# x loaded into the slots of the residual sums, Exp put right behind Ln, and RWKV pairs with grouped y products and joint key transposes

## The chip, the cores and the metric

The kernel runs on one core of one Trainium2 chip. The metric is the device time of one execution in microseconds; less is better. The times of before are those of three runs.

## What is computed

The reference runs two blocks on x (512 rows of 1024 columns), in fp32. Only the first block is touched. Its core:

```python
mod = silu(c) @ ada_w + ada_b
shift, scale, gate = split(mod, 3)
h = rmsnorm(x, norm_g) * (1.0 + scale) + shift
p = h @ w_in
y_rwkv = rwkv7_group(p[..., :RWKV_COLS], ...)     # 8 heads of 64
y_sb = stick_breaking_group(p[..., RWKV_COLS:], sb_norm_g)   # 8 heads of 64
y = concatenate([y_rwkv, y_sb]) @ w_out
x = x + gate * y
return rmsnorm(x, final_g)
```

`rwkv7_group` carries a 64x64 state per head over the 512 positions:

```python
sa = einsum('bhij,bhj->bhi', state, -kk_t)
state = state * w_t + sa * b_t + v_t * k_t
y_t = einsum('bhij,bhj->bhi', state, r_t)
```

The second block (two layers, the first with a short convolution and a second stream `ctx` of 256 rows, the second with neighbourhood attention, both with a feed-forward part) follows on the result.

## The kernel before, in words

Activations lie with the columns on the partitions (8 k-tiles of 128 by 512 positions). The large fp32 products (GEMMs) are made of three products each, with operands cut into a high and a low part (L172 to L174): per output tile of 128 columns and k-tile three matmuls of 512 positions. `fetch` (L165 to L168) loads weights on SP's queue into `st` (two buffers), ScalarE makes the high part `wh` (L155), VectorE the low part `wl` (L156), four buffers each.

Eight heads of each kind are worked off in pairs. `rwkv_pair` computes the recurrence by chunks of 64 positions, in NCH = 8 steps; `sb_pair` the stick-breaking attention in four row blocks of 128, the last of 512 columns. Their order is the tuple ORDER (L21): an RWKV pair is a generator that is advanced in three pieces, and stick-breaking pairs stand between. The program's text sets only priorities: a list scheduler of the Tile framework puts the instructions of each engine in one fixed order, so that pieces of several pairs, GEMMs among them, stand interleaved. Each engine's queue is worked in that order.

In an RWKV pair the two heads e = 0, 1 lie on partitions 0 to 63 and 64 to 127 (`hs[e]`). The keys of each head are transposed chunk by chunk (L1031) into `BK[e]`. Then come the steps: first state product (L1057, L1059), solve (L1064), new state (L1070, L1074 to L1077), and the output of the step: per head a product of 128 rows (L1081, `SV` by `MMt`), and one of 64 rows (L1083, the old state `VS` by `RA`), which add up in PSUM bank `py`. L1086 copies the bank; L1088, L1093 and L1098 are the norm's sums, and L1099 to L1102 end the pair. `rsqrt` (L240) makes Ln (L242) and Exp (L248) on ScalarE; these two lie in one activation table, the sigmoids of the stick-breaking blocks in another, and each change loads a table.

PSUM banks in the first block: `acc` two (GEMMs), `sm`, `sc`, `py`, `ss`, `sp` and `so` one each.

The output projection goes by eight column blocks m. For each the first six k-tiles (y0, y4, y1, y5, y2, y6, in the order YORD) are multiplied while the last RWKV pair (y3) and the last stick-breaking pair (y7) are still running; for m = 0 to 5 the sum is put out of PSUM at L421 as `part` = sum * gate + x, into the slot of a y that has been split (L307) into its high and low part. x comes from six tiles `xt` of the pool "tail" (L402 to L404), which is opened in the space of the closed pool `rk`, the RWKV pairs' working tiles: a load waits until the tile that lay there is read out. m = 6 and 7 stay in PSUM. Then `w_out2` brings the last two k-tiles (y3, y7) of all eight blocks (L444 to L452), and L461 takes the first sum of squares of the next norm. Beside it the contexts of the second block are loaded (`xc`, L407) and modulated (`nt`, L287; `hc`, L288 to L290).

Of the kernel before, what the change touches and what calls it, by code (L numbers as in the profile page):

```python
# [8 lines left out]
F32 = mybir.dt.float32  # L9
F32R = mybir.dt.float32r  # L10
BF16 = mybir.dt.bfloat16
AF = mybir.ActivationFunctionType
# [5 lines left out]
S = 512  # L18
# [4 lines left out]
CH = 64  # L23
NCH = S // CH
YORD = (0, 4, 1, 5, 2, 6, 3, 7)
# [59 lines left out]
class K:  # L85
# [154 lines left out]
    def rsqrt(self, t, ps, after=None, scale=1.0, eps=0, since=None, out=None, view=None):  # L240
        nc = self.nc
        i = nc.scalar.activation(t, ps, AF.Ln, scale=scale, bias=self.eps[:, eps:eps + 1])  # L242
        if after is not None:
            self.order(i, self.table(after))
        if since is not None:
            self.order(i, since)
        src, dst = (t, t) if out is None else (view[1](t), view[0](out))
        return nc.scalar.activation(dst, src, AF.Exp, scale=-0.5)  # L248

    def sumsq(self, xs, n, pool, tag, psum, scale=None):  # L250
        nc = self.nc
# [57 lines left out]
    def block1(self):  # L309
        nc, tc, A = self.nc, self.tc, self.A  # L310
# [8 lines left out]
        y = [None] * 8  # L319
# [3 lines left out]
        with self.open(name="n1", bufs=2) as npool:  # L323
# [16 lines left out]
            for ch in range(4):  # L340
                pm = self.psum(("py", "sp")[ch % 2])
                for kp in range(4):
                    st = npool.tile([128, 2, 512], F32, tag="ast", name="ast", bufs=16)
                    nc.sync.dma_start(st, A["ada_n"][ch, kp])
                    for i in range(2):
                        k = 2 * kp + i
                        r = slice(32 * (k % 4), 32 * (k % 4) + 32)
# [4 lines left out]
                for i in range(4):  # L352
                    nc.tensor.matmul(tr[:, j + i:j + i + 1], lhsT=ev[:, 128 * i:128 * i + 128], rhs=self.C("sel"),
                                     start=True, stop=True)
# [23 lines left out]
        with self.open(name="sb", bufs=1) as sb:  # L378
            with self.open(name="rk", bufs=1) as rk:
                self.rk, self.sb = rk, sb  # L380
                pl = pre[12]
                zl = rk.tile([128, S], F32, name="zl")
                self.mix(pl, self.V("mu", 12), omu[:, 12:13], zl)
                nc.scalar.activation(zl[0:64], zl[0:64], AF.Tanh)
                self.y = y
                runs = [self.rwkv_pair(p, W, h, zl, omu, oka, pre) for p in range(4)]
                for n in ORDER[:-1]:
                    if n < 4:
                        next(runs[n], None)
                    else:  # L390
                        y[n] = self.sb_pair(n - 4, W, h, sb)
            self.xp = self.pool("xp", side="right")
            self.cxp = self.pool("cxp", side="right")
            self.hcp = self.pool("hc", side="right")
            self.xas = ExitStack()
            xa = self.xas.enter_context(self.open(name="xa", bufs=1, side="right"))
            y[7] = self.sb_pair(3, W, h, sb)
            if self.dbg:
                for k in range(8):
                    nc.sync.dma_start(A['dbg_y'][k], y[k])  # L400
            with self.open(name="tail", bufs=2) as tp:
                xts = [tp.tile([128, S], F32, name=f"xt{m}", bufs=1) for m in range(6)]  # L402
                for m in range(6):
                    nc.sync.dma_start(xts[m], A["x"][m // 2, :, m % 2])  # L404
                xc = self.xc = [self.cxp.tile([128, SC], F32, tag=f"xc{k}", name=f"xc{k}") for k in range(KT)]
                for k in range(KT):
                    nc.sync.dma_start(xc[k], A["ctx"][k])  # L407
                hc = self.hc = [self.hl(self.hcp, SC, f"hc{k}") for k in range(KT)]
                gc = self.gain("gc0", "norm_mix0", mod, 8, 1)
                pc = self.psum("py")[:, :SC]  # L410
                self.sumsq(xc, SC, tp, "c", pc)
                rstd = tp.tile([128, SC], F32, name="rstd", bufs=1)
                since = self.rsqrt(rstd, pc, since=self.sbexp)
                self.modulate(xc, range(KT), gc, mod, 0, 1, hc, tp, "cz", rstd)
                yh, part = [], []
                for k in YORD:
                    if k == 3:
                        for m in range(6):
                            po = self.xgemm(A["w_out"][m], yh, 0, 6)
                            t = self.yp.tile([128, S], F32, tag=f"y{YORD[m]}", name="part")  # L420
                            nc.vector.scalar_tensor_tensor(t, po, self.m1[:, 16 + m, 0:1], xts[m],  # L421
                                                           op0=ALU.mult, op1=ALU.add)
                            part.append(t)
                        for m in (6, 7):
                            po = self.psum("acc")
                            self.gemm(po, A["w_out"][m], yh, 0, 6, last=False)
                            part.append(po)
                        w2 = self.load_w(A["w_out2"][0], 1024) + self.load_w(A["w_out2"][1], 1024)
                    t = self.hl(self.hp, S, f"h{k}")
                    self.split(t, y[k])  # L430
                    yh.append(t)
        xs = self.xs = [xa.tile([128, S], F32, tag=f"x{k}", name=f"x{k}") for k in range(KT)]
        for k in (6, 7):
            nc.sync.dma_start(xs[k], A["x"][k // 2, :, k % 2])
# [10 lines left out]
        for n, m in enumerate((6, 7, 0, 1, 2, 3, 4, 5)):  # L445
            po, base = (part[m], xs[m]) if m >= 6 else (self.psum("acc"), part[m])
# [13 lines left out]
            if n >= 5:  # L460
                nc.tensor.matmul(ms, lhsT=self.C("ones") if n == 5 else fwt[:, n - 6], rhs=acc if n == 5 else sq,  # L461
                                 start=n == 5, stop=n == 7)
# [443 lines left out]
    def rwkv_pair(self, p, W, h, zl, omu, oka, pre):  # L906
        nc, rk = self.nc, self.rk
        TT, STT = nc.vector.tensor_tensor, nc.vector.scalar_tensor_tensor
        mm = nc.tensor.matmul
# [3 lines left out]
        sm = lambda: self.psum("sm", name="rsm")  # L913
# [17 lines left out]
        sg, a = T("t1"), T("t2")  # L931
# [18 lines left out]
        f = T("t1")  # L950
        nc.vector.tensor_scalar(f, a, self.V("k_a", p), oka[:, p:p + 1], op0=ALU.mult, op1=ALU.add)
        XY = T("XY", (128, NCH, 2, CH), 2)
        RA = T("RA", (128, NCH, 2, CH), 2)
        tb = T("tb", bufs=2)
        for e in range(2):
            r = slice(64 * e, 64 * e + 64)
# [8 lines left out]
        MMt = [T(f"MM{e}", (128, NCH, CH), 2) for e in range(2)]  # L965
# [5 lines left out]
        hs = [slice(0, 64), slice(64, 128)]  # L971
        for e in range(2):
            ro, rt = hs[e], hs[1 - e]
# [13 lines left out]
        for c in range(NCH):  # L987
            for q in range(4):
                ro, cl = hs[q // 2], slice(32 * (q % 2), 32 * (q % 2) + 32)
# [34 lines left out]
        TT(XY, XY, PP[:, :, CH:CH + 1].unsqueeze(3).to_broadcast([128, NCH, 2, CH]), ALU.mult)  # L1024
        yield
        BK = [T(f"BK{e}", (128, NCH, CH)) for e in range(2)]
        for e in range(2):
            ro = hs[e]
            pB = self.psum("sm", (128, NCH, CH), "pB")
            for c in range(NCH):  # L1030
                nc.tensor.transpose(pB[:, c], XY[ro, c].rearrange("p a t -> p (a t)"),  # L1031
                                    self.C("ident")[ro, 64 * e:64 * e + 64])
            nc.scalar.copy(BK[e], pB)
        VS = [T(f"VS{e}", (128, NCH, CH)) for e in range(2)]
        SV = [T(f"SV{e}", (128, NCH, CH)) for e in range(2)]
        for w0 in range(0, 9, 4):
# [10 lines left out]
            nc.scalar.copy(VS[1][0:64, w0 - 1 + s0:w0 + n - 1], pV[0:64, s0:n, 64:128])  # L1047
            nc.scalar.copy(SV[1][0:64, w0 - 1 + s0:w0 + n - 1], pV[0:64, s0:n, 64:128])

        pY = self.psum("py")  # L1050
        slots = self.psum("sc", (128, 8, CH))
        for c in range(NCH):
            pR = slots[:, (3 * c + 0) % 8]
# [13 lines left out]
            if c < NCH - 1:  # L1067
# [3 lines left out]
                for e in range(2):  # L1071
# [3 lines left out]
                    else:  # L1075
                        STT(VS[e][r, c + 1], VS[e][r, c], PP[r, c, CH:CH + 1], pS[r],
                            op0=ALU.mult, op1=ALU.add)  # L1077
            for e in range(2):
                r = hs[e]
                o = pY[r, c * CH:c * CH + CH]  # L1080
                mm(o, lhsT=SV[e][:, c], rhs=MMt[e][:, c], start=True, stop=c == 0)  # L1081
                if c > 0:
                    mm(o, lhsT=VS[e][r, c], rhs=RA[r, c, 0, :], start=False, stop=True)  # L1083

        ys = T("BK0")
        nc.scalar.copy(ys, pY)  # L1086
# [188 lines left out]
```

## Time and profile before

| | us |
|---|---|
| median of three runs | 2110.76 |
| lowest and highest | 2107.98, 2111.87 |
| profiled execution, its own time | 2105.49 |
| its span in the trace | 2103.7 |
| TensorE busy | 2051.8 (98%) |
| VectorE busy | 1231.9 (59%) |
| ScalarE busy | 795.2 (38%) |
| GpSimd busy | 131.5 (6%) |
| mean HBM traffic | 96 GB/s |
| mean granted TensorE clock | 0.986 |

The trace is that of one execution, which was 5.3 us faster than the median. Its span lacks 1.8 us of its time, what lies ahead of the first and behind the last recorded instruction. A row of the table of windows shows for a stretch of the span the busy time and the count of instructions of each engine; a row of the timeline shows start, duration, engine, line and operation (and in brackets the idle time before it, with what ended it). A row of the groups shows busy time, mean duration of one, and the idle time before.

### The profile page before, as it was taken

What the parts mean: (1) busy time and instruction counts of PE and PEld (TensorE: products, weight loads), DVE (VectorE), ACT (ScalarE), POOL (GpSimd) and SP (SyncE); (2) the same over time, 40 slices, a digit from 0 to 9 for tenths busy, and PEclk for the clock granted to TensorE, in tenths of its full rate; (3) what the DMA queues carried; (4) which work ended last, traced back from release to release, by engine and by line L of the source; (5) the groups of instructions that cost most, each with busy time, mean ns of one, the idle gap of its engine ahead of it and who ended that gap; (6) DMA issues with size and microseconds to landing.
All of it is one profiled execution on the core that took longest, in us unless ns stands there. A gap on an engine that the chain in (4) does not pass through costs nothing.

```text
span 2103.7 us, 33543 instructions
## 1 busy us (share of the span) xinstructions
PE 2051.8 (98%) x13596; PEld 1651.6 (79%) x13596; DVE 1231.9 (59%) x2641; ACT 795.2 (38%) x1485; POOL 131.5 (6%) x212
## 2 busy tenths in 40 slices
PE   6999999998999999999999999999999999999999
PEld 3766666655888888888888888898777787888887
DVE  2969887645777756767456443354566655434443
ACT  3536444345422224221222122244777744323232
POOL 0000000000000000001001000000233200000000
PEclk9999999987999999999999999999999999999999
DMA  7432313112243421445234322222111122333333
GB/s 279 147 111 83 111 53 98 40 56 81 71 129 122 130 81 45 147 127 174 90 123 155 114 91 60 61 81 71 43 59 61 36 66 92 95 100 96 94 99 102
DMA packets 61356, 203.60 MB, mean 97 GB/s; under 512 B 6928, under 2 KB 8976, under 8 KB 61200
## 3 DMA queue, kind: packets, MB, share of 16 engines
q1 hardware_dynamic: 45360, 145.77, 21.3%
q0 software_dynamic: 15120, 55.06, 8.1%
q8 instruction: 107, 1.75, 0.3%
q10 hardware_dynamic: 720, 0.62, 0.1%
q14 instruction: 49, 0.40, 0.1%
HBM read 199.32 MB, written 2.10 MB: 96 GB/s over the span
## 4 chain that ended last, share of the span: by engine, by line
PE 87%; ACT 3%; DVE 3%; issue 1%; POOL 0%; POOLq 0%; ACTq 0%; DVEq 0%
PE acc L173 19%; PE acc L172 19%; PE acc L174 19%; PE cacc L174 5%; PE cacc L173 5%; PE cacc L172 5%; PE py L895 2%; PE pT L875 2%; PE ss L1147 1%; PE so L1169 1%; PE sm L862 1%; PE py L1083 1%; PE sm L863 1%; PE py L1081 1%; PE ss L1162 1%
## 5 line engine op out<-in xcount | busy, mean ns | idle before, releaser
L155 ACT CAST wh<-st 128x512 fp32r<-128x512 f32 (+2 forms) x481 | 292.3, 609 | 729.8 <-PE acc L173 287.7
L156 DVE TENSOR_TENSOR wl<-st,wh 128x512 fp32r<-128x512 f32 (+2 forms) x481 | 323.1, 674 | 353.9 <-ACT wh L155 350.7
L172 PE MATMUL acc<-xzzh,wh 128*128 128x512 f32 x352 | 138.8, 394 | 0.0
L174 PE MATMUL acc<-xzzh,wl 128*128 128x512 f32 x352 | 138.1, 392 | 0.0
L173 PE MATMUL acc<-xzzl,wh 128*128 128x512 f32 x352 | 138.0, 392 | 0.0
L210 DVE CUSTOM_DVE_ANT_0 junk<-ast,cb,vec 128x512 bf16<-128x512 f32 x168 | 125.2, 745 | 14.5 <-DMA ast<-in_w_ada_dram 11.9
L210 DVE CUSTOM_DVE_ANT_0 junk<-ast,cb,m 128x512 bf16<-128x512 f32 x168 | 125.5, 747 | 2.8
L200 POOL DMA_DIRECT2D ast<-in_w_ada_dram x96 | 50.6, 528 | 1022.3 <-DVE m L210 957.2
L174 PEld LDWEIGHTS acc<-xzzh,wl 128*128 128x128 f32 x352 | 66.0, 188 | 14.8
L172 PEld LDWEIGHTS acc<-xzzh,wh 128*128 128x128 f32 x352 | 66.1, 188 | 13.6 <-issue 0.5
L173 PEld LDWEIGHTS acc<-xzzl,wh 128*128 128x128 f32 x352 | 66.1, 188 | 13.4 <-issue 0.5
L172 PE MATMUL acc<-h0h,wh 128*128 128x512 f32 (+1 forms) x164 | 65.8, 401 | 6.0 <-DVE part L421 3.1
L173 PE MATMUL cacc<-czzl,wh 128*128 128x256 f32 x240 | 68.1, 284 | 0.0
L172 PE MATMUL cacc<-czzh,wh 128*128 128x256 f32 x240 | 67.7, 282 | 0.0
L174 PE MATMUL cacc<-czzh,wl 128*128 128x256 f32 x240 | 67.3, 280 | 0.0
L174 PE MATMUL acc<-h2h,wl 128*128 128x512 f32 (+1 forms) x164 | 65.8, 401 | 0.0
L173 PE MATMUL acc<-h1l,wh 128*128 128x512 f32 (+1 forms) x164 | 65.7, 401 | 0.0
L173 PE MATMUL acc<-h3l,wh 128*128 128x512 f32 (+1 forms) x164 | 65.3, 398 | 0.3 <-DVE h3l L290 0.3
L173 PE MATMUL acc<-h6l,wh 128*128 128x512 f32 (+1 forms) x164 | 65.5, 399 | 0.1
L173 PE MATMUL acc<-h0l,wh 128*128 128x512 f32 (+1 forms) x164 | 65.4, 399 | 0.0
L174 PE MATMUL acc<-h0h,wl 128*128 128x512 f32 (+1 forms) x164 | 65.3, 398 | 0.1
L174 PE MATMUL acc<-h1h,wl 128*128 128x512 f32 (+1 forms) x164 | 65.2, 398 | 0.0
(731 smaller groups left out, 5576.1 us busy)
## 6 DMA issues: line engine op xcount, KB each, us to landing
ast<-in_w_ada_dram POOLq DMA_DIRECT2D x96, 512.0 KB, 3.8
st<-in_ffn_w_in_dram SPq DMA_DIRECT2D x88, 512.0 KB, 3.4
st<-in_ffn_w_out_dram SPq DMA_DIRECT2D x32, 448.0 KB, 3.3
st<-in_w_in_dram SPq DMA_DIRECT2D x24, 512.0 KB, 3.5
st<-in_conv_w_in_dram SPq DMA_DIRECT2D x24, 512.0 KB, 3.6
ast<-in_ada_n_dram SPq DMA_DIRECT2D x16, 512.0 KB, 9.0
st<-in_ffn_w_out_dram SPq DMA_DIRECT2D x16, 512.0 KB, 3.5
st<-in_w_qk_dram SPq DMA_DIRECT2D x16, 512.0 KB, 3.5
```

The lines of the kernel that those rows point to most:

```text
L155: nc.scalar.copy(hi[:, :n], sl)
L156: nc.vector.tensor_tensor(lo[:, :n], sl, hi[:, :n].bitcast(F32), ALU.subtract)
L172: mm(out, lhsT=lh, rhs=rh, start=first, stop=False)
L173: mm(out, lhsT=lh, rhs=rl, start=False, stop=False)
L174: return mm(out, lhsT=ll, rhs=rh, start=False, stop=last)
L200: self.nc.gpsimd.dma_start(st, src)
L210: i = self.nc.vector.tensor_tensor_reduce(out=junk, in0=st[:, hs], in1=c[:, hs], scale=0.5, scalar=o if hf else self.V(bname, j), op0=ALU. ...
L862: mm(o, lhsT=qh[:, e, qs], rhs=ks, start=True, stop=False)
L863: mm(o, lhsT=ql[:, e, qs], rhs=ks, start=False, stop=True)
L875: nc.tensor.transpose(pT[:, to], s[:, 128 * i:128 * i + 128], self.C("ident"))
L895: self.nc.tensor.matmul(po[r, cs], lhsT=v[:, r], rhs=pts[e][:, blk:blk + n].rearrange("p a t -> p (a t)"), start=i == 0, stop=i == len(wor ...
L1081: mm(o, lhsT=SV[e][:, c], rhs=MMt[e][:, c], start=True, stop=c == 0)
```

## The change

Four edits, all in the first block:

1. In `rsqrt` the Exp is issued at high priority, so that the scheduler may set it right behind its Ln.
2. The six `xt` tiles and their loads are gone. Right behind the split of the k-th y (k in YORD) the slot of that y is taken as `part`, and x is loaded into it (L431); the evacuation (L418) reads x there and writes the sum in its place.
3. The keys of both heads are transposed at once: two groups of four 128x128 transposes, and four copies of 256 columns, in place of sixteen 64x128 transposes and two copies of 512.
4. The y products are written behind the steps c = 3 and 7, for four steps at a time: first all products of 128 rows (L1082), then all of 64 rows (L1085). In the PSUM bank only the first step's product starts a sum and only the last step's product ends it.

```diff
-        return nc.scalar.activation(dst, src, AF.Exp, scale=-0.5)
+        with self.tc.high_priority():
+            return nc.scalar.activation(dst, src, AF.Exp, scale=-0.5)
...
-                xts = [tp.tile([128, S], F32, name=f"xt{m}", bufs=1) for m in range(6)]
-                for m in range(6):
-                    nc.sync.dma_start(xts[m], A["x"][m // 2, :, m % 2])
...
-                            t = self.yp.tile([128, S], F32, tag=f"y{YORD[m]}", name="part")
-                            nc.vector.scalar_tensor_tensor(t, po, self.m1[:, 16 + m, 0:1], xts[m],
+                            nc.vector.scalar_tensor_tensor(part[m], po, self.m1[:, 16 + m, 0:1], part[m],
                                                            op0=ALU.mult, op1=ALU.add)
-                            part.append(t)
...
                     yh.append(t)
+                    m = len(part)
+                    if m < 6:
+                        t = self.yp.tile([128, S], F32, tag=f"y{k}", name="part")
+                        nc.sync.dma_start(t, A["x"][m // 2, :, m % 2])
+                        part.append(t)
...
-        for e in range(2):
-            ro = hs[e]
-            pB = self.psum("sm", (128, NCH, CH), "pB")
-            for c in range(NCH):
-                nc.tensor.transpose(pB[:, c], XY[ro, c].rearrange("p a t -> p (a t)"),
-                                    self.C("ident")[ro, 64 * e:64 * e + 64])
-            nc.scalar.copy(BK[e], pB)
+        for hf in range(2):
+            pB = self.psum("sm", (128, 4, 2, CH), "pB")
+            for c in range(4):
+                nc.tensor.transpose(pB[:, c].rearrange("p a t -> p (a t)"),
+                                    XY[:, 4 * hf + c].rearrange("p a t -> p (a t)"), self.C("ident"))
+            for e in range(2):
+                nc.scalar.copy(BK[e][:, 4 * hf:4 * hf + 4], pB[:, :, e])
...
-            for e in range(2):
-                r = hs[e]
-                o = pY[r, c * CH:c * CH + CH]
-                mm(o, lhsT=SV[e][:, c], rhs=MMt[e][:, c], start=True, stop=c == 0)
-                if c > 0:
-                    mm(o, lhsT=VS[e][r, c], rhs=RA[r, c, 0, :], start=False, stop=True)
+            if c % 4 == 3:
+                for d in range(c - 3, c + 1):
+                    for e in range(2):
+                        mm(pY[hs[e], d], lhsT=SV[e][:, d], rhs=MMt[e][:, d], start=d == 0, stop=False)
+                for d in range(max(c - 3, 1), c + 1):
+                    for e in range(2):
+                        mm(pY[hs[e], d], lhsT=VS[e][hs[e], d], rhs=RA[hs[e], d, 0, :], start=False, stop=d == NCH - 1)
```

The scheduler moves instructions with it. Three places:

SP's queue at the end of the first block, before (`st` are weights, `xt` and `x` tiles of x, `xc` of the contexts):

```order
L167 DMA st<-in_w_out_dram 128x768 x6
L404 DMA xt_5143<-in_x_dram 128x512
L404 DMA xt_5144<-in_x_dram 128x512
L404 DMA xt_5145<-in_x_dram 128x512
L404 DMA xt_5146<-in_x_dram 128x512
L404 DMA xt_5147<-in_x_dram 128x512
L404 DMA xt_5148<-in_x_dram 128x512
L407 DMA xc_5155<-in_ctx_dram 128x256
```

and after, with the six loads into `part`:

```order
L167 DMA st<-in_w_out_dram 128x768 x3
L431 DMA part<-in_x_dram 128x512 x6
L167 DMA st<-in_w_out_dram 128x768 x5
L405 DMA xc_5119<-in_ctx_dram 128x256
L405 DMA xc_5120<-in_ctx_dram 128x256
```

The x loads stand three w_out loads earlier, ahead of five of them and of the contexts; x6 and x7 (L434, now L435), which stood behind the contexts, now come behind the two loads of w_out2.

TensorE at the last step of the last RWKV pair, before (`py` is the bank of y, `ss` and `so` belong to the stick-breaking pair, `rsm` to the norm):

```order
L1081 MATMUL py<-MM_4259,SV_4683 64x64
L1083 MATMUL py<-RA,VS_4681 64x64
L1081 MATMUL py<-MM_4260,SV_4684 64x64
L1083 MATMUL py<-RA,VS_4682 64x64
L1162 MATMUL ss<-con,sg 128x128
L1088 MATMUL rsm<-BK_4831,con 128x512
L1147 MATMUL ss<-qk_4901,qk_4864 128x384
```

and after:

```order
L1082 MATMUL py<-MM_4242,SV_4660 64x64
L1085 MATMUL py<-RA,VS_4657 64x64
L1085 MATMUL py<-RA,VS_4658 64x64
L1085 MATMUL py<-RA,VS_4657 64x64
L1085 MATMUL py<-RA,VS_4658 64x64
L1085 MATMUL py<-RA,VS_4657 64x64
L1085 MATMUL py<-RA,VS_4658 64x64
L1085 MATMUL py<-RA,VS_4657 64x64
L1085 MATMUL py<-RA,VS_4658 64x64
L174 MATMUL acc<-h6h,wl 128x512
L1165 MATMUL ss<-con,sg 128x128 x3
L172 MATMUL acc<-h0h,wh 128x512
```

The products of 64 rows of four steps stand together, those of 128 rows still in or right behind their own steps, and products of the output projection (`acc`) stand between where there were none: from the pair's first state product to its first norm sum there are 75 GEMM products, before 42.

VectorE behind the last stick-breaking pair (`ors` and `y` end the pair, `nt` and `hc` are the contexts, h7l is the low part of y7), before:

```order
L1177 SCALAR_TENSOR_TENSOR ors<-so,vec,ors 128x512
L287 SCALAR_TENSOR_TENSOR nt<-xc_5155,gc_5187,rstd 128x256
L1180 TENSOR_TENSOR y_5138<-ors,sgs 128x512
L287 SCALAR_TENSOR_TENSOR nt<-xc_5156,gc_5187,rstd 128x256
L290 SCALAR_TENSOR_TENSOR hc0l<-nt,m_0_70,hc0h 128x256
L421 SCALAR_TENSOR_TENSOR part<-acc,m_69,xt_5146 128x512
```

and after:

```order
L291 SCALAR_TENSOR_TENSOR hc2l<-nt,m_0_70,hc2h 128x256
L291 SCALAR_TENSOR_TENSOR hc3l<-nt,m_0_70,hc3h 128x256
L288 SCALAR_TENSOR_TENSOR nt<-xc_5123,gc_5151,rstd 128x256
L288 SCALAR_TENSOR_TENSOR nt<-xc_5124,gc_5151,rstd 128x256
L308 TENSOR_TENSOR h7l<-y_5114,h7h 128x512
L291 SCALAR_TENSOR_TENSOR hc4l<-nt,m_0_70,hc4h 128x256
L291 SCALAR_TENSOR_TENSOR hc5l<-nt,m_0_70,hc5h 128x256
L288 SCALAR_TENSOR_TENSOR nt<-xc_5125,gc_5151,rstd 128x256
L288 SCALAR_TENSOR_TENSOR nt<-xc_5126,gc_5151,rstd 128x256
L452 SCALAR_TENSOR_TENSOR x_5523<-acc,m_69,x_5523 128x512
```

Before, three evacuations (L421) stood among the contexts, and h7l behind all of them; now no evacuation of the first six k-tiles is left here, h7l stands in the middle of the contexts, and the last sums (L452) among the rest.

More of the change, by code (lines that the diff above doesn't have):

```diff
@@ L1048, in rwkv_pair @@
             nc.scalar.copy(SV[1][0:64, w0 - 1 + s0:w0 + n - 1], pV[0:64, s0:n, 64:128])
-        pY = self.psum("py")
+        pY = self.psum("py", (128, NCH, CH))
         slots = self.psum("sc", (128, 8, CH))
@@ L1077, in rwkv_pair @@
                             op0=ALU.mult, op1=ALU.add)
-            for e in range(2):
-                r = hs[e]
-                o = pY[r, c * CH:c * CH + CH]
-                mm(o, lhsT=SV[e][:, c], rhs=MMt[e][:, c], start=True, stop=c == 0)
-                if c > 0:
-                    mm(o, lhsT=VS[e][r, c], rhs=RA[r, c, 0, :], start=False, stop=True)
+            if c % 4 == 3:
[5 more added lines that the diff above has]
+                        mm(pY[hs[e], d], lhsT=VS[e][hs[e], d], rhs=RA[hs[e], d, 0, :], start=False, stop=d == NCH - 1)
+        pY = pY.rearrange("p c t -> p (c t)")
         ys = T("BK0")
```

## The prediction

> **What bounds the kernel now.** The page comes first (span, share of TensorE), then the table of windows, by which the first block is cut at three borders: A, the last RWKV pair's first state product (429.1 us); B, its first norm sum (468.8); U, the last value product of the last stick-breaking pair (502.1). The end, C, is the first sum of squares behind the output projection (536.7); behind it TensorE's order of instructions is the same in both kernels.
>
> ```profile
> span 2103.7 us, 33543 instructions
> 60.00:429.10 369.10, 359.67 (x4345) 248.67 (x4343) 289.68 (x693) 170.86 (x329) 15.82 (x30) 1.00 0.28 90
> 429.10:468.80 39.70, 37.36 (x237) 23.00 (x236) 19.63 (x60) 14.79 (x41) 0.00 (x0) 0.85 0.20 64
> 468.80:502.10 33.30, 26.07 (x76) 12.87 (x76) 15.05 (x25) 15.09 (x26) 0.00 (x0) 0.56 0.18 56
> 502.10:536.70 34.60, 33.55 (x143) 26.52 (x143) 26.84 (x56) 19.01 (x36) 0.00 (x0) 1.00 0.30 99
> 453.60:489.30 35.70, 26.18 (x105) 12.35 (x103) 12.73 (x30) 14.19 (x25) 0.00 (x0) 0.55 0.32 100
> ```
>
> In each row stand the stretch, then busy time and count of TensorE, its weight loads, VectorE, ScalarE and GpSimd, then TensorE's granted clock. Up to A TensorE is busy for 359.67 of 369.10 us at full clock: there every TensorE microsecond saved moves the end. From 453.6 to 489.3 it is different: clock 0.55, and no product of the large GEMMs in the list. The timeline shows why:
>
> ```profile
> 452.01 0.40 PE L174 MATMUL acc<-h6h,wl 128*128 128x512 f32 x1
> 453.54 26.22 SPq L404 DMA_DIRECT2D xt<-in_x_dram  x6
> 478.71 0.69 DVE L1099 TENSOR_TENSOR tb<-vm,rsm 128x512 f32<-128x512 f32 x1 [7.13 <-PE rsm L1098]
> 488.51 0.72 DVE L421 SCALAR_TENSOR_TENSOR part<-acc,m,xt 128x512 f32<-128x512 f32 x1
> 489.29 0.79 PE L172 MATMUL acc<-h0h,wh 128*128 128x512 f32 x1 [3.07 <-DVE part L421]
> ```
>
> By 452.0 two column blocks of the output projection fill both `acc` banks. They are emptied by L421, which needs `xt`. The six `xt` loads take until 479.8 to be issued, since `xt` lies in the space of the closed RWKV pool and the last reader there, `tb` (L1099), ran at 478.7; and in VectorE's order L421 stands behind the end of the last pair. So TensorE has only the pair's own small products for 35.7 us, at half clock, and the other six blocks (108 products of 512 columns) come behind.
>
> **The change part by part.**
>
> *Y products.* One step of one pair, before:
>
> ```profile
> 163.80 0.33 PE L1081 MATMUL py<-MM,SV 128*64 128x64 f32 x2
> 164.06 0.33 PE L1083 MATMUL py<-RA,VS 64*64 64x64 f32 x2
> 164.31 0.33 PE L1081 MATMUL py<-MM,SV 128*64 128x64 f32 x2
> 164.57 0.33 PE L1083 MATMUL py<-RA,VS 64*64 64x64 f32 x2
> 451.35 0.33 PE L1064 MATMUL sc<-Rh,Z 64*64 64x64 f32 x4
> 451.61 0.33 PE L1162 MATMUL ss<-con,sg 128*128 128x128 f32 x1
> 453.14 0.28 PE L1081 MATMUL py<-MM,SV 128*64 128x64 f32 x2
> 453.35 0.33 PE L1083 MATMUL py<-RA,VS 64*64 64x64 f32 x2
> ```
>
> Starts lie 0.25 to 0.26 us apart, so each of the four products costs 0.26, and a pair costs 7 steps of 1.03 and one of 0.52: 7.7 us. Each changes the shape of the array (128 rows, 64 rows, 128 rows). Two products of one shape in a row, both heads', are L1064 x4: 0.26 for two, 0.13 each. After the change the 14 state products (L1085) come as 6 and 8 of one shape: 14 x 0.13 = 1.8, perhaps 1.0. The 16 others (L1082) still stand in their own steps: 0.21 behind a product of their shape (453.14 to 453.35), 0.26 alone, so 3.4 to 4.2. Sum 4.4 to 6.0, taken as 5.0: 2.7 us less per pair (1.7 to 3.3).
>
> *Transposes of the keys.*
>
> ```profile
> 119.22 0.71 PE L1031 MATMUL pB<-con,XY 64*128 64x64 f32 x8
> 119.86 0.50 PE L173 MATMUL acc<-h1l,wh 128*128 128x512 f32 x1
> 120.89 0.60 PE L1041 MATMUL pV<-con,vm 128*128 128x128 f32 x4
> 121.25 0.48 PE L174 MATMUL acc<-h2h,wl 128*128 128x512 f32 x1
> ```
>
> Eight take 0.64; four of 128x128, the new form, 0.36. Twice each: 1.28 against 0.72, 0.6 us less per pair. ScalarE gets four copies of 256 columns for two of 512; it is busy for 171 of 369 us up to A, which hides them. If that cover were gone, two more copies per pair at under 0.6 us each.
>
> Three pairs ahead of A: 3 x 3.3 = 9.9 us. The new order puts four more GEMM products ahead of A, 4 x 0.225 (222 in 50 us, next row) = 0.9. So **A comes 9.0 earlier**, at 420.1 (3 to 12).
>
> ```profile
> 1850.00:1900.00 50.00, 50.00 (x222) 41.43 (x221) 20.07 (x31) 14.09 (x24) 0.00 (x0) 1.00 0.29 95
> 122.10:165.70 43.60, 11.54 (x27) 5.09 (x27) 1.00 0.25 85
> 236.80:282.30 45.50, 9.24 (x21) 4.01 (x21) 1.00 0.26 83
> 326.40:366.80 40.40, 14.71 (x40) 7.51 (x40) 1.00 0.27 91
> 429.10:468.80 39.70, 6.07 (x14) 2.65 (x14) 0.85 0.20 64
> ```
>
> *x in the slots, A to B.* The last four rows are the same stretch of all four pairs, with the products of L172 alone, a third of the GEMM's. The first three pairs hide 81, 63 and 120 products in 43.6, 45.5 and 40.4 us; the last, without evacuations, only 42 in 39.7. After the change a `part` load needs only the split of one y, of which the sixth is early (h6l, next rows), and L418 stands in VectorE's order within the steps: 75 products before the norm sum. I take **41** us, the mean of the three, 43, less the 3 us of y products, and 1 for the softmax between them (37 to 46).
>
> ```profile
> 436.86 0.66 DVE L307 TENSOR_TENSOR h6l<-y,h6h 128x512 fp32r<-128x512 f32 x1
> 476.56 1.28 ACT L1152 ACT_TABLE_LOAD   x1
> 506.63 1.11 DVE L1180 TENSOR_TENSOR y<-ors,sgs 128x512 f32<-128x512 f32 x1
> 536.74 1.12 PE L461 MATMUL ss<-acc,con 128*128 128x512 f32 x2 [0.45 <-DVE acc L459]
> L156 DVE TENSOR_TENSOR wl<-st,wh 128x512 fp32r<-128x512 f32 (+1 forms) x12 | 7.2, 618 | 3.2 <-ACT wh L155 3.2
> L451 DVE SCALAR_TENSOR_TENSOR x<-acc,m,part 128x512 f32<-128x512 f32 x6 | 4.4, 743 | 0.0
> L459 DVE SCALAR_TENSOR_TENSOR acc<-sq,fw,acc 128x512 f32<-128x512 f32 x5 | 3.7, 744 | 0.3 <-ACT sq L454 0.3
> L287 DVE SCALAR_TENSOR_TENSOR nt<-xc,gc,rstd 128x256 f32<-128x256 f32 x8 | 3.6, 477 | 0.1
> L290 DVE SCALAR_TENSOR_TENSOR hc0l<-nt,m,hc0h 128x256 fp32r<-128x256 f32 x1 | 0.5, 476 | 0.0
> ```
>
> *B to U.* 26.07 us of TensorE at clock 0.56 would be 14.6 at full clock; behind it stands the chain through sigmoid, scan and transposes of two 512-column blocks. With GEMM products between, the clock should hold. I take **24** us (20, TensorE's 14.6 with half of the idle 7.2 and 2 for table loads; 30, if the clock stays at half for most of it).
>
> *U to C.* Before, 108 GEMM products stand between B and the first product of the last two k-tiles; after, 71. TensorE has little left here: 8 blocks x 6 x 0.225 = 10.8 and some 4 from before. VectorE has, by the groups: `ors` 0.8, y 1.1, eight `nt` 3.6, eight `hcl` 3.8, four `wl` 2.5, h7l 0.7, eight evacuations 6.0, six `acc` 4.2, the rest 0.9: 23.6, and its order now puts four hcl and six nt ahead of h7l, about 12 us behind U, for which TensorE waits some 6. With the wait for the rsqrt I take **27** us (22 to 33), against 34.6: VectorE becomes the bound here.
>
> The clock: in 453.6 to 489.3 it was 0.55 although TensorE is listed busy for 26.18 of 35.7 us and waited at most 3.07 ahead of a GEMM product. The Trainium skill ("TensorE: Matmul & The Clock Gate", Part 1) puts the half clock behind an idle window of about 3.4 us and lets 3.4 us of work end it; the trace shows half clock without a listed wait that long. By the page's rule the wait for h7l costs half of 3.4 us of products, which VectorE's bound hides: 27 stays. By the trace's half clock throughout, 42 products (48 without the first two blocks' products with y3) take 19 us instead of 9.5, against VectorE's 15 behind h7l: 31.
>
> *Exp behind Ln.* In the order a sigmoid still stands between the last pair's Ln and Exp, and there are 34 table loads in both: nothing; at most one load of 1.28 either way. The x6 and x7 loads move behind those of w_out2 on SP's queue; they are needed only at the first evacuation behind h7l, so nothing.
>
> *Sum.* C = 420.1 + 41 + 24 + 27 = 512.1 against 536.7: **24.6 us less**; behind C nothing. The profiled execution took 2105.5 (span 2103.7), so it would take 2080.9; on the median of the runs shown, 2110.8, it is **2086**. If all terms fell at their ends: 39 less or 1 less.
>
> **The rivals.**
>
> *Gain given back behind U.* The evacuations come earlier, but the last stick-breaking pair sets U, and VectorE's contexts stand ahead of h7l. For it: U to C was full before because GEMM work was left. With half clock, B to U 30 and U to C 35, A gaining 5: 424 + 41 + 30 + 35 = 530, 7 less: 2104. Against it: VectorE's sum is only 23.6.
>
> *Grouped products don't overlap.* Both heads' products write one PSUM bank, from row tiles 0 and 64. If one waited for the other, each would keep 0.26: 14 x 0.26 + 4.2 = 7.8, no saving on y, 8 us over three pairs: 2094. That would follow from a rule of the Trainium skill ("TensorEngine Tiling (Array Packing)", Restrictions and Gotchas, Gotcha 1): different row tiles can't access one PSUM bank at once. The trace speaks against it: L1064 x4 writes one bank from both row tiles and takes 0.26 in all.
>
> *Slower: weights stuck behind x.* SP issues in order, and the six `part` loads, each waiting for VectorE's split of one y, now stand ahead of five w_out loads. If the split of y6 came late, block 3 and all behind it would start late, and L418, now within the recurrence's VectorE order, would hold the steps. TensorE asks for block 3 about 20 us behind A (three blocks, 54 x 0.225 = 12, and about half of the pair's own products, 8); the split was 7.7 behind A (436.86). From 20 on each microsecond counts. With the four last blocks pushed behind B, 72 products at half clock: 420 + 45 + 45 + 35 = 545, 8 more: 2119. Against it: 12 us of slack.
>
> *The change doesn't do what it says* holds for the Exp edit, counted above.
>
> **How the numbers follow.** Forecast 0.73; gain given back 0.13; no overlap 0.09; slower 0.05. The predicted time is the forecast's, 2086. The range, 2072 to 2106, takes in the terms' ends on the fast side, 39 less, the no-overlap case and the given-back case; the slower case is left out, and some of the tails. About 0.2%, 4.2 us, is what a measurement of this kernel can tell from no change. Within it lies about half of the given-back case: 0.06. Faster is the forecast, no overlap and the other half: 0.89. Slower 0.05.
>
> **What would show it.** Right: the state products in groups of 6 and 8 with starts about 0.1 us apart; last pair's first state product near 420; w_out products between it and the norm sum, granted clock near 1 from 440 to 490; `part` loads issued before 430; first sum of squares near 512; then the same 1567 us to the end. Wrong: groups at 0.26 a product; a wait of TensorE on `wh` of block 3; clock 0.5 behind U; or a longer stretch behind C.

## The result, and the profile after

The changed kernel took 2079.43 us (median of four runs, 2076.49 to 2084.22) beside 2109.37 of before: 29.9 less, a ratio of 0.9864 (0.9842 to 0.9887). In a second series it was 2081.57 beside 2108.59, 0.9874 (0.9843 to 0.9905). The prediction was 2086 on a before of 2110.8, 24.6 less. The profiled execution took 2080.14, 25.35 less than the profiled one of before.

The table of windows of the changed kernel, cut at the same borders: up to A (first state product of the last RWKV pair), to B (its first norm sum), to U (last value product of the last stick-breaking pair), to C (first sum of squares).

```profile
span 2078.4 us, 33492 instructions
60.00:421.30 361.30, 350.87 (x4317) 242.29 (x4315) 290.29 (x694) 171.69 (x338) 15.83 (x30) 0.99 0.29 93
421.30:462.50 41.20, 41.20 (x277) 25.61 (x277) 24.81 (x69) 16.98 (x46) 0.00 (x0) 1.00 0.21 64
462.50:485.90 23.40, 22.98 (x109) 15.27 (x108) 15.18 (x26) 16.30 (x28) 0.00 (x0) 1.00 0.43 130
485.90:510.90 25.00, 19.58 (x68) 13.83 (x67) 20.36 (x42) 15.00 (x27) 0.00 (x0) 0.86 0.21 64
```

The stretches, in us:

| | before | forecast | after |
|---|---|---|---|
| A at | 429.1 | 420.1 | 421.3 |
| A to B | 39.7 | 41 | 41.2 |
| B to U | 33.3 | 24 | 23.4 |
| U to C | 34.6 | 27 | 25.0 |
| C at | 536.7 | 512.1 | 510.9 |
| C to the end of the span | 1567.0 | 1567 | 1567.5 |

The clock, 0.55 from 453.6 to 489.3 before, is 1.00 from A to U, and TensorE is busy for nearly all of it. What made that possible, and what is left, in the timeline:

```profile
414.44 14.83 SPq L431 DMA_DIRECT2D part<-in_x_dram  x6
461.01 0.68 PE L1085 MATMUL py<-RA,VS 64*64 64x64 f32 x16
461.62 0.51 PE L174 MATMUL acc<-h6h,wl 128*128 128x512 f32 x1
491.09 0.87 DVE L288 SCALAR_TENSOR_TENSOR nt<-xc,gc,rstd 128x256 f32<-128x256 f32 x2
496.24 0.69 DVE L308 TENSOR_TENSOR h7l<-y,h7h 128x512 fp32r<-128x512 f32 x1
496.99 0.80 PE L173 MATMUL acc<-h7l,wh 128*128 128x512 f32 x1 [4.13 <-DVE h7l L308]
510.88 1.12 PE L462 MATMUL ss<-acc,con 128*128 128x512 f32 x2 [0.27 <-DVE acc L460]
```

The x loads are all issued by 429.3 instead of 479.8. Eight state products (two passes each) take 0.61 us, 0.076 each. Behind U TensorE waits 4.13 us for the low part of y7, which stands on VectorE behind six context tiles, and it ends waiting for VectorE's sums. From the end of the pair (489.27) to C VectorE itself waits only 0.81 and 0.45 us: it is the bound there, as forecast. The joint transposes, four at a time:

```profile
118.79 0.66 PE L1031 MATMUL pB<-con,XY 128*128 128x128 f32 x4
119.21 0.47 PE L172 MATMUL acc<-h0h,wh 128*128 128x512 f32 x1
120.22 0.63 PE L1031 MATMUL pB<-con,XY 128*128 128x128 f32 x4
120.60 0.47 PE L173 MATMUL acc<-h1l,wh 128*128 128x512 f32 x1
```

0.42 and 0.38 us, 0.80 for a pair in place of 1.28.

### The profile page after: what moved, and what is told of

The parts are those of the page before. It is cut to its first block, busy times and chain, and to the rows that moved or that the text cites. A ratio compares the mean times of both kernels' runs of the same rounds, so it can differ in the third digit from the quotient of the medians.

```text
span 2078.4 us, 33492 instructions
## 1 busy us (share of the span) xinstructions
PE 2029.1 (98%) x13564; PEld 1637.2 (79%) x13564; DVE 1230.9 (59%) x2641; ACT 795.6 (38%) x1493; POOL 131.5 (6%) x212
## 4 chain that ended last, share of the span: by engine, by line
PE 87%; ACT 3%; DVE 3%; issue 1%; POOL 0%; DMA 0%; POOLq 0%; DVEq 0%; ACTq 0%
PE acc L173 20%; PE acc L174 20%; PE acc L172 19%; PE cacc L174 5%; PE cacc L173 5%; PE cacc L172 5%; PE py L896 2%; PE pT L876 1%; PE ss L1150 1%; PE so L1172 1%; PE sm L863 1%; PE sm L864 1%; PE G L980 1%; DVE nt L288 1%; PE ss L1165 1%
## 5 line engine op out<-in xcount | busy, mean ns | idle before, releaser
L174 PEld LDWEIGHTS acc<-xzzh,wl 128*128 128x128 f32 x352 | 66.0, 188 | 14.8
L173 PE MATMUL acc<-h7l,wh 128*128 128x512 f32 (+1 forms) x164 | 65.2, 397 | 4.1 <-DVE h7l L308 4.1
L172 PE MATMUL acc<-h3h,wh 128*128 128x512 f32 (+1 forms) x164 | 65.1, 399 | 0.9 <-DVE x L452 0.9
L174 PE MATMUL acc<-h7h,wl 128*128 128x512 f32 (+1 forms) x164 | 65.1, 397 | 0.4 <-issue 0.4
L173 PE MATMUL acc<-h5l,wh 128*128 128x512 f32 (+1 forms) x164 | 65.4, 399 | 0.0
```

The lines of the kernel that those rows point to most:

```text
L172: mm(out, lhsT=lh, rhs=rh, start=first, stop=False)
L173: mm(out, lhsT=lh, rhs=rl, start=False, stop=False)
L174: return mm(out, lhsT=ll, rhs=rh, start=False, stop=last)
```

## The experiments

The theory is that of the prediction: two gains that add up, TensorE time taken away ahead of the last pair, and its empty half-clock stretch filled with the projection's products. The rivals: that only the clock is won, that the parts pay only together, that the heads' products don't overlap, that TensorE and not VectorE sets the end.

**The slots alone.** Before with edit 2 only.

```diff
-                xts = [tp.tile([128, S], F32, name=f"xt{m}", bufs=1) for m in range(6)]
-                for m in range(6):
-                    nc.sync.dma_start(xts[m], A["x"][m // 2, :, m % 2])
...
+                        t = self.yp.tile([128, S], F32, tag=f"y{k}", name="part")
+                        nc.sync.dma_start(t, A["x"][m // 2, :, m % 2])
+                        part.append(t)
```

> Before with the slots alone: x loaded into the slots of the split y's, y products, transposes and Exp as before. Theory (the gap behind the two full accumulators is filled): the last pair's first state product stays at 429; 67 instead of 42 GEMM products stand between it and the norm sum, so that stretch takes about 43 (the earlier pairs' 40 to 45); norm sum to last value product about 25 instead of 33, at a clock near 1; from there to the first sum of squares about 27 instead of 35. Together 12 less, about 2097 on the scale of before's 2109. Rival A (only the clock is gained, products merely change place): about 8 less. Rival B (the slots pay only together with the cheaper pairs): under 4 less.

Measured: 2092.25 (2087.55 to 2096.33) beside 2108.70, 16.5 less where 12 was forecast, ratio 0.9918 (0.9899 to 0.9938). From its A (437.7) on:

```profile
437.70:479.35 41.65, 41.65 (x267) 25.64 (x267) 24.39 (x68) 16.56 (x45) 0.00 (x0) 1.00 0.22 71
479.35:500.20 20.85, 20.41 (x99) 13.06 (x97) 13.76 (x23) 13.34 (x25) 0.00 (x0) 1.00 0.33 106
500.20:525.49 25.29, 22.07 (x92) 16.62 (x92) 22.58 (x45) 16.44 (x30) 0.00 (x0) 1.00 0.26 84
```

A to C takes 87.8 us instead of 107.6: 19.8 less, more than the whole change gains there (89.6, so 18.0). So the slots need no help from the pairs' edits, and rival B falls. Rival A has its price too low (8), but not its mechanism. If the length of each stretch is multiplied by its granted clock, A to C is 87.0 us before and 87.8 here. By this count the slots take no work off TensorE: the products change place, and what is won is the clock, 0.85 and 0.56 in the first two stretches before and 1.00 now.

The profiled A came 8.6 later than before's, although TensorE's order up to it is the same. The windows of the first pair's preparation show why:

```profile
112.30:115.70 3.40, 1.93 (x39) 1.68 (x39) 1.87 (x3) 3.16 (x6) 0.43 (x2) 1.00 0.70 239
115.70:132.70 17.00, 17.00 (x91) 13.86 (x91) 6.98 (x15) 3.59 (x9) 0.75 (x2) 0.50 0.30 94
```

The clock was at half for 17 us, though TensorE is listed busy throughout: 8.5 us lost. Runs of one kernel differ by such stretches: the four runs had mean clocks of 0.992, 0.996, 0.992 and 0.993, and the one of 0.996 took 2087.55.

**The pairs' edits alone.** Before with edits 3 and 4.

```diff
-        for e in range(2):
-            ro = hs[e]
-            pB = self.psum("sm", (128, NCH, CH), "pB")
...
+        for hf in range(2):
+            pB = self.psum("sm", (128, 4, 2, CH), "pB")
...
+            if c % 4 == 3:
+                for d in range(c - 3, c + 1):
```

> Before with the two edits of the RWKV pairs alone (grouped y products, joint transposes); x stays in its own tiles. Theory (TensorE time is taken away ahead of the last pair, and little in the stretch at half clock): first state product of the last pair 8 earlier, as in the change; that pair's stretch 2 shorter; the rest as before. Together 10 less, 2099. With the slots' 12 this makes 22 of the change's 25 to 30. Rival (the gain ahead of the last pair is lost in the wait for x, since the load's issue hangs on the end of the pair): this end moves along with the pair, so the rival too gives 8 to 10 less; told apart by the issue of the last x load, 479.4 before: 469 to 470 by the theory, unmoved by a rival that ties it to something else.

Measured: 2094.41 (2091.41 to 2097.98), 14.3 less where 10 was forecast, 0.9925 (0.9907 to 0.9942). In the profile A lies at 422.9, 6.2 earlier, and A to C takes 103.6, 4.0 less; the last pair's own stretch, forecast 2 shorter, takes 40.0 and is not. SP's queue:

```profile
442.79 29.09 SPq L404 DMA_DIRECT2D xt<-in_x_dram  x6
```

The x loads now end at 471.9 instead of 479.8: their issue moves with the pair's end. 16.5 and 14.3 are 30.8: the gains add up to the change's 29.9, within the scatter.

**The y products alone.** Edit 4 in before.

```diff
-            for e in range(2):
-                r = hs[e]
-                o = pY[r, c * CH:c * CH + CH]
...
+            if c % 4 == 3:
+                for d in range(c - 3, c + 1):
```

> Before with the grouped y products alone. By the terms of the prediction 2.7 less for each of the three pairs ahead of the last, 8 less there, and 1 to 2 in the last pair: 9 to 10 less, 2100. If the products of 64 rows were held up by their common PSUM bank: no difference, 2109.

Measured: 2097.78 (2094.03 to 2107.55, ten runs), 10.9 less, 0.9952 (0.9938 to 0.9967). As forecast. In the profiled run, which took 2102.05, TensorE had half clock in the third pair's preparation:

```profile
312.00:320.00 8.00, 6.93 (x175) 4.30 (x175) 6.41 (x17) 2.91 (x5) 1.06 (x2) 1.00 0.40 131
320.00:336.00 16.00, 16.00 (x80) 10.19 (x81) 9.31 (x21) 7.12 (x14) 0.53 (x1) 0.57 0.22 68
```

**The joint transposes alone.** Edit 3 in before.

```diff
-        for e in range(2):
-            ro = hs[e]
-            pB = self.psum("sm", (128, NCH, CH), "pB")
...
+        for hf in range(2):
+            pB = self.psum("sm", (128, 4, 2, CH), "pB")
```

> Before with the joint transposes alone. By the prediction 0.6 for each pair, 1.8 ahead of the last pair's first state product, less 0.9 for four GEMM products that its order moves ahead: 1 to 2 less, 2107 to 2108. If ScalarE's two more copies per pair cost what they take (0.4 each, on the path): no difference or 1 more.

Measured: 2118.03 (2112.83 to 2119.20, five runs), 9.3 more, 1.0035 (1.0021 to 1.0048). Both numbers were missed: a saving of TensorE time made the kernel slower. The windows of this kernel:

```profile
298.00:304.00 6.00, 3.72 (x84) 2.87 (x82) 5.93 (x13) 2.85 (x6) 0.00 (x0) 0.99 0.27 83
304.00:317.00 13.00, 13.00 (x158) 9.73 (x159) 7.45 (x17) 2.65 (x6) 0.00 (x0) 0.50 0.14 45
```

and of before, over the latter stretch:

```profile
304.00:317.00 13.00, 10.97 (x314) 7.82 (x314) 10.52 (x31) 2.75 (x5) 0.53 (x1) 1.00 0.40 124
```

With the edit the scheduler places the third pair's preparation otherwise. From 298 to 304 TensorE is busy for 3.72 of 6 us, its longest wait 1.32; then its clock is at half for 13 us, in which it is listed busy throughout: 6.5 us lost. That is half of the 13.7 us by which this profiled run (2119.20) exceeds before's. The rest is half clock as well: over the whole span it costs 44.5 us here and 29.5 in before (span times one minus the mean clock, 0.979 and 0.986). ScalarE's two more copies are no explanation: it is busy for 2.65 of those 13.

**The changed kernel again**, the reference for the next three:

> The changed kernel itself, beside the next three on the same chip. 25 to 30 less than before: 2079 to 2084, a ratio of 0.986 to 0.988.

Measured: 2081.57 (2078.32 to 2088.50), as expected. A to C took 89.7, the same as in the first profile; A lay at 424.4, 3.1 later.

**The products of each head together.** In the changed kernel the two loops around the products of 64 rows are exchanged.

```diff
-                for d in range(max(c - 3, 1), c + 1):
-                    for e in range(2):
+                for e in range(2):
+                    for d in range(max(c - 3, 1), c + 1):
                         mm(pY[hs[e], d], lhsT=VS[e][hs[e], d], rhs=RA[hs[e], d, 0, :], start=False, stop=d == NCH - 1)
```

> The changed kernel with the grouped products of 64 rows ordered by head: three or four of one head (one row tile), then those of the other, instead of in turn. If the heads' products overlap because they lie in different row tiles, eight products take 8 x 0.13 = 1.0 us and more instead of 0.61, about 0.8 us more per pair, 2 to 3 us in all. If only the change of shape had cost time, no difference (within 0.5 us, and 0.61 us for eight). If products of different row tiles had to wait for each other at their common bank, this order is the faster one, by 1 us or more.

Measured: 2083.97 (2082.82 to 2085.39), 2.4 more than the changed kernel, with overlapping intervals (0.9857 to 0.9906 against 0.9843 to 0.9905). The timeline decides:

```profile
468.32 0.96 PE L1085 MATMUL py<-RA,VS 64*64 64x64 f32 x16
469.21 0.50 PE L174 MATMUL acc<-h6h,wl 128*128 128x512 f32 x1
```

Eight products take 0.89 us instead of 0.61. The single records show the overlap: in turn, the sixteen passes start in pairs 0.006 us apart, behind the first a pair every 0.058; by head one pass starts every 0.058, and the heads run side by side for the four passes in which the second has begun and the first has not ended. So products of the two row tiles overlap in one PSUM bank; that is worth 0.28 for eight, about 0.5 us per pair. The larger part of the gain, from 0.26 to 0.11 each, came with the grouping, with little of the overlap.

**The split of y7 ahead.** In the changed kernel:

```diff
-                    self.split(t, y[k])
+                    if k == 7:
+                        with tc.high_priority():
+                            self.split(t, y[k])
+                    else:
+                        self.split(t, y[k])
```

> The changed kernel with the split of the last y at high priority: on VectorE its low part comes behind two of the eight context tiles instead of six, so TensorE's wait of 4.13 us for it shrinks to about 1. If VectorE's sum of work sets the stretch from the last value product to the first sum of squares (25.0 us, VectorE idle for 1.3 of it behind the first wait), 0 to 1.3 less. If TensorE's wait and the half clock behind it set it, 4 to 7 less.

Measured: 2079.83 (2076.11 to 2082.28), 1.7 less than the changed kernel beside it, not clear of the intervals (0.9834 to 0.9886). U to C took 24.0, 1.0 less:

```profile
497.74 0.50 PE L173 MATMUL acc<-h7l,wh 128*128 128x512 f32 x1 [0.38 <-DVE h7l L308]
502.19 0.80 PE L172 MATMUL acc<-h3h,wh 128*128 128x512 f32 x1 [3.27 <-DVE x L456]
```

The wait of 4.13 shrank to 0.38, and another of 3.27 for VectorE's evacuation took its place a block later. So VectorE's sum sets this stretch. The run doesn't take the half clock away: it is 0.86 from U to C here too.

**The contexts on GpSimd.** In the changed kernel the context's two element-wise steps go to GpSimd, with one ScalarE pass more for each tile (gain and shift are applied on ScalarE).

```diff
+            if eng is not None:
+                eng.tensor_tensor(t, xs[k], rstd, ALU.mult)
+                nc.scalar.activation(h[k][0], t, AF.Identity, bias=mod[:, sh0 + k, r:r + 1], scale=gain[:, k:k + 1])
...
+                nc.scalar.activation(u, t, AF.Identity, bias=mod[:, sh0 + k, r:r + 1], scale=gain[:, k:k + 1])
+                eng.tensor_tensor(h[k][1], u, h[k][0].bitcast(F32), ALU.subtract)
```

> The changed kernel with the first layer's context modulation taken off VectorE: the two element-wise steps on GpSimd, with one more pass of ScalarE for each tile. 7.3 us of VectorE's work goes from the stretch behind the last value product, and the low part of y7 comes right behind y. If VectorE's sum sets that stretch, it shrinks from 25.0 to about 18 (TensorE's 48 products, 10.8, behind y7), and the whole by 5 to 7, if GpSimd's 16 steps take under 0.9 us each; if they take longer, the contexts come late for the next GEMM and part of it is lost. If TensorE and the clock set it, 4 to 7 less as well, but then the run before this one gives the same.

Measured: 2087.40 (2084.09 to 2093.01), 5.8 more than the changed kernel, 0.9900 (0.9865 to 0.9934); U to C 30.1. Missed.

```profile
491.29 2.33 POOL L289 TENSOR_TENSOR nt<-xc,rstd 128x256 f32<-128x256 f32 x2 [127.86 <-ACT rstd L249]
491.87 2.30 DVE L156 TENSOR_TENSOR wl<-st,wh 128x512 fp32r<-128x512 f32 x2
494.72 0.72 POOL L289 TENSOR_TENSOR nt<-xc,rstd 128x256 f32<-128x256 f32 x1
503.95 0.79 PE L172 MATMUL acc<-h7h,wh 128*128 128x512 f32 x1 [11.20 <-ACT h7h L314]
```

On ScalarE's queue the high part of y7 stood behind all context passes, which wait for GpSimd, and TensorE behind that for 11.2 us. Two splits of VectorE took 1.15 us each beside GpSimd, where 0.69 was usual, and GpSimd's two products beside them 1.17, where 0.72 was.

**Two repairs of it.** The split of y7 ahead too, and then, of the two context steps, only the second on GpSimd:

```diff
-            nc.vector.scalar_tensor_tensor(h[k][1], t, sh, h[k][0].bitcast(F32),
-                                           op0=ALU.add, op1=ALU.subtract)
+            if eng is not None:
...
+                nc.scalar.activation(u, t, AF.Identity, bias=sh)
+                eng.tensor_tensor(h[k][1], u, h[k][0].bitcast(F32), ALU.subtract)
```

> The kernel of contexts_on_gpsimd with the split of the last y at high priority too. There TensorE waited 11.2 us for the high part of y7, which stood on ScalarE's queue behind context passes that wait for GpSimd; now it stands ahead of them. If that queue alone spoiled the run, the stretch from the last value product to the first sum of squares falls from 30 to 22 or 23 (it was 25.0 in the changed kernel), and the whole is 2 to 3 less than the changed kernel: 2077 to 2079. If GpSimd's work itself costs VectorE its speed (a 128x512 split took 1.15 us beside it instead of 0.69), no more than the changed kernel's time is reached: 2080 to 2083.

> The same with the first context step (eight products of 0.48 us) left on VectorE and only the low parts on GpSimd (eight of 0.69). VectorE has 3.8 us less than in the changed kernel, ScalarE eight passes more (4 us). By VectorE's sum: the stretch 25.0 to about 21.5, 3 less than the changed kernel, 2077. If ScalarE's squares, which now stand behind sixteen context passes, set the end: 24, so 1 less, 2080.

Measured: 2082.65 (2079.94 to 2086.72) and 2082.80 (2079.27 to 2083.52), beside 2107.61: 0.9889 (0.9872 to 0.9905) and 0.9880 (0.9867 to 0.9893). No gain over the changed kernel; U to C 26.2 and 25.9. The first lies within its second forecast (2080 to 2083), the second misses both of its own. The waits of TensorE in the first, with the squares on ScalarE, and in the second:

```profile
PE ss L473 <- DVE acc L471: 7.4, 1, 7.4
499.63 2.19 ACT L466 ACTIVATE sq<-x 128x512 f32<-128x512 f32 x4
```

```profile
PE ss L471 <- DVE acc L469: 4.9, 1, 4.9
```

The projection's products are now done early, but VectorE's sums wait for ScalarE's squares, which stand behind sixteen context passes (in the first run until 499.63), and then fill the rest of the stretch: part of the bound went from VectorE to ScalarE. In the first run GpSimd's work also slows VectorE's splits beside it (1.17 and 1.21 us). Of these versions none is clearly faster than the changed kernel; the split of y7 ahead is the only one on the right side of it.

**The changed kernel without the joint transposes**, and **the transposes alone once more**:

```diff
-        for hf in range(2):
-            pB = self.psum("sm", (128, 4, 2, CH), "pB")
...
+        for e in range(2):
+            ro = hs[e]
+            pB = self.psum("sm", (128, NCH, CH), "pB")
```

> The changed kernel with the transposes of each head as before. If the joint transposes save what TensorE's rows say, 0.6 for each pair: 1 to 2.5 more than the changed kernel, 2082 to 2084. If what the transposes edit alone showed (9 more) came with the edit itself, this kernel is the faster one, by up to 9: 2072. If that came from the granted clock (half from 304 to 317 in that run's profile), the difference to the changed kernel follows the clock in the profile: within 4 either way, with a stretch of half clock named beside it.

> The kernel of the run e4 (joint transposes alone) once more, on another occasion. If the 9 us lie in the edit's own order, its profile shows TensorE at half clock in the third pair's preparation (about 300 to 320) again, and the median is again 2113 to 2119 beside before's 2108. If the episode came by chance, the profile's half clock lies elsewhere or lacks, and the median is 2106 to 2109.

Measured: 2091.44 (2085.62 to 2100.07, six runs) beside 2107.61, 0.9928 (0.9907 to 0.9950): without the transposes the change gains 16.2 instead of 27 to 30. All three forecasts (1 to 2.5 more than the changed kernel, up to 9 less, within 4) are missed. Its profiled run, the slowest of the six (2100.07), lost its time ahead of A (440.2); from there to C it took 88.6. Two stretches ahead of A:

```profile
120.00:130.00 10.00, 10.00 (x51) 8.07 (x50) 5.45 (x12) 1.96 (x4) 0.53 (x1) 0.50 0.28 101
332.00:344.00 12.00, 12.00 (x55) 7.31 (x53) 6.68 (x14) 4.06 (x8) 0.53 (x1) 0.54 0.12 44
```

The transposes alone took 2115.54 (2107.29 to 2122.37, nine runs) beside 2107.61, 1.0028 (1.0004 to 1.0052), and the half clock lay at the same place, on another chip:

```profile
302.00:316.00 14.00, 13.73 (x161) 10.28 (x161) 8.74 (x22) 2.81 (x6) 0.00 (x0) 0.53 0.15 52
```

So this belongs to that kernel's order and not to chance alone. Its nine runs have mean clocks from 0.977 to 0.985, in the order of their times: 2122.37 at 0.977, 2107.29 at 0.985, where before's runs of that clock took 2106.1 to 2108.3. In the same way the fastest run without joint transposes (2085.62) had 0.992, where the changed kernel took 2078.73, 2084.22 and 2083.04: 1 to 7 less. So the 8 to 10 us by which kernels with and without the joint transposes differ, with the sign depending on the other edits, go with the clock.

A count over all runs separates the two. Span times mean clock is the span with half clock counted half; the rest is what half clock cost, waits in it included. Means over the runs of each kernel, in us:

| | runs | span times clock | lost to half clock |
|---|---|---|---|
| before | 35 | 2074.1 | 33.2 |
| slots alone | 4 | 2076.2 | 14.1 |
| pairs' edits alone | 4 | 2065.5 | 27.2 |
| y products alone | 10 | 2067.0 | 30.0 |
| transposes alone | 14 | 2073.4 | 40.6 |
| changed kernel | 8 | 2064.6 | 14.8 |
| changed, without the transposes | 6 | 2066.5 | 24.1 |

Runs of one kernel scatter by 1 to 2 us in span times clock (standard deviation). By this count the slots won clock alone and the y products mostly work. The joint transposes won 1 us of work alone and 2 in the changed kernel, and moved the cost of half clock by 7 and 9, once up and once down.

The Exp edit had no run of its own, so its share isn't shown. The other edits alone add up to the whole change, which leaves little for it.

## Why the prediction was right, and where it was off

- **What bounds the kernel** held: the half-clock stretch vanished as the loads came early, and the slots alone gave 19.8 us between A and C. By the count above all of that is the clock, which the products in between keep up; no run has the clock up without them.
- **Y products**: 2.7 us per pair was the forecast, from 0.13 for each state product; they take 0.076. Alone the edit gave 10.9, against some 10 forecast; by the count 7.1 of it is work and the rest the clock, so that the match is in part luck.
- **Transposes**: 0.56 for a pair was forecast, 0.48 is in the rows; the sum counts three pairs ahead of A, where those of all four pairs lie. But to add this saving to the sum left out a term: that a new order can set off stretches of half clock elsewhere. Alone the edit was slower by 8 to 9 us.
- **A**: 9.0 forecast, 7.8 in the first profile, 4.7 in the second. Up to A TensorE's busy time fell by 8.8 us (359.67 to 350.87), as forecast with 9.9 less 0.9; the rest are waits and clock.
- **A to B, B to U**: 41 and 24 forecast, 41.2 and 23.4 measured, at clock 1.00.
- **U to C**: 27 forecast, 25.0 measured. VectorE was busy for 20.4 us where 23.6 had been summed up (the durations listed in the stretch add up to 23.9): its instructions overlap, as these rows of the changed kernel show, in which starts lie 0.66 us apart and each is listed with 0.74. The sum of durations was the mis-sized term.

```profile
508.77 0.74 DVE L460 SCALAR_TENSOR_TENSOR acc<-sq,fw,acc 128x512 f32<-128x512 f32 x1
509.43 0.74 DVE L452 SCALAR_TENSOR_TENSOR x<-acc,m,part 128x512 f32<-128x512 f32 x1
510.09 0.74 DVE L460 SCALAR_TENSOR_TENSOR acc<-sq,fw,acc 128x512 f32<-128x512 f32 x1
```

The clock fell to 0.86 in this stretch, and VectorE hid most of the loss: it waited for TensorE only 1.3 us between the pair's end and C.
- **Gain given back behind U**: its place was right (contexts ahead of h7l, a wait of 4.13, half clock), its price wrong: B to U needed 23.4 and not 30.
- **No overlap**: refuted by 0.61 against 0.89 us for eight products. The rule of the Trainium skill ("TensorEngine Tiling (Array Packing)", Gotcha 1), that different row tiles can't access one PSUM bank at once, doesn't hold as a wait here, where the two heads write different partitions of the bank.
- **Weights stuck behind x**: the x loads were all issued by 429.3, and from A to U TensorE waited for no weights.
- **The clock**: in the transposes' run it fell behind 6 us with 3.72 busy and no wait over 1.32, and stayed at half for 13 us in which TensorE is listed busy without a gap. By the Trainium skill ("TensorE: Matmul & The Clock Gate", Part 1) half clock comes behind an idle window of about 3.4 us, and full clock behind 3.4 us of work. Of this the traces show the length: each of the 85 stretches of half clock that lie within the spans of the fourteen traces lasts 3.41 us or a whole multiple of it. This one of before lasts 41.0, twelve times as long.

```profile
457.10:498.00 40.90, 32.21 (x99) 15.62 (x100) 16.60 (x32) 15.01 (x26) 0.00 (x0) 0.50 0.21 67
```

They don't show the two conditions, if idle and work are read from the listed busy time. What counts as either, no run here tells.

The forecast gave about 12 us to the pairs' edits (9.0, and 3 in the last pair) and 12.6 to the slots; alone they gave 14.3 and 16.5. The two profiled executions differ by 25.35, the medians by 29.9 and 27.0. By the count the change is 9.5 us of work and 18.4 of clock: the work came out under the pairs' 12, the clock over the slots' 12.6, and the two misses partly cancel. The ends of the prediction's own terms add up to 41 and 2 less, not to 39 and 1.

What stays open: what ends a stretch of half clock, and why some orders meet one in most runs. The order alone doesn't decide it: up to A the slots' kernel has before's order of TensorE, and near 115 us one had 17 us of half clock, the other 3.4.

## What to carry to other kernels

Where both accumulators are full, look for what keeps them from being emptied: here six small loads waited for space of a pool that was still being read, and a slot that was free 50 us earlier was worth 16 to 20 us, by keeping TensorE supplied and its clock up. Price a saving on the busy engine by the products it removes, but expect a rearranged order to move the cost of half clock by several microseconds either way. Before an effect of 0.4% is put down to the work removed, split it by span times mean clock; the median is still what the kernel costs. Where an engine other than TensorE bounds a stretch, taking one wait away shows whether another of the same engine takes its place.

## What the runs showed of the hardware

- Half clock came only in whole multiples of 3.41 us (85 stretches): 13.7 us in the transposes' runs, 17.1 in the slots' run, 41.0 in before. It stayed at half while TensorE was listed busy throughout (17.00 of 17.00 us, 13.00 of 13.00). Mean clock and time go together: from 0.977 to 0.985 in one kernel, 15 us.
- Products of 64 rows in opposite row tiles overlap within one PSUM bank: eight in 0.61 us in turn, with starts in pairs 0.006 us apart, and in 0.89 by tile.
- Where VectorE's 128x512 split and GpSimd's 128x256 product ran side by side, the split took 1.15 us instead of 0.69, and the product 1.17 instead of 0.72.
